# Reading the first octet of K and V in pieces of 32 KB, in a linear ReLU attention kernel

## Chip, cores and metric

The kernel runs on one core of one Trainium2 chip. The metric is the device time of one execution in microseconds; the median of 3 runs is 126.92 us (126.89 to 127.21).

## What is computed

The inputs Q, K and V are fp32 arrays of 8 batches x 12 heads x 512 rows x 64 columns, and so is the output: 96 heads, 12.58 MB for each array.

```python
Q_feat = np.maximum(0, Q)
K_feat = np.maximum(0, K)
KV = np.einsum('bhkd,bhkv->bhdv', K_feat, V)
K_sum = np.sum(K_feat, axis=2)
numerator = np.einsum('bhqd,bhdv->bhqv', Q_feat, KV)
denominator = np.einsum('bhqd,bhd->bhq', Q_feat, K_sum)
return (numerator / (denominator[:, :, :, None] + 1e-10)).astype(np.float32)
```

## The kernel before

The 96 heads are cut into 12 octets of eight heads. One octet of one input is 1 MB of fp32 that lies in one run of DRAM; seen as 128 partitions, each partition holds 32 rows of 64 values, 8 KB. For each octet the kernel forms KV and the column sums on TensorE (`mm_kv`, L185 to L190, or `mm_kv8`, L160 to L168, for the first octet), transposes and clips Q (`transp`, `relu_q`), multiplies (`out_t`, `denom`), transposes back (`back`), divides (`norm`, L271) and stores (`store`, L277 to L287).

The loads come in two kinds.

- Q of every octet, and K and V of octets 1 to 11, are loaded by GpSimd (L97 to L105), with the cast from fp32 to bf16 made on the way. K and V come in two halves per octet, called groups, so an octet takes five such DMAs: Q 512 KB and four of 256 KB, as written. All of them are issued in one list at the start of GpSimd's program (L113 to L118): Q of octet 0 first, then K, V, K, V, Q of octet 1, and so on. GpSimd gets through the list as earlier transfers land and buffers come free.
- K and V of octet 0 (tiles `k8` and `v8`, named k_first and v_first in the profile) come as fp32 without a cast, 1 MB each. K is issued by SyncE (L111) and V by ScalarE (L112), as the first DMA of each engine.

From `k8` VectorE makes the clipped and masked bf16 operands (L152), from `v8` ScalarE (L156) and VectorE (L157) make the others; this is `prep8` (L148 to L158). TensorE's list begins with the transposes of Q of octet 0 (L208), and the 32 matmuls of `mm_kv8` (L163) come after them. Then the loop over the octets runs as written out by hand from L322 on.

SyncE's queue holds, after K of the first octet, the stores in order. Each of the first seven stores stands behind a tiny DMA (L280) that reads some rows of a K group five octets further on, so that SyncE issues the store only once that group has landed; the first store is issued at 44.02 us of the span. The last octet is stored in two halves (L285).

Of the kernel before, what the change touches and what calls it, by code (L numbers as in the profile page):

```python
# [10 lines left out]
def kernel(  # L11
# [7 lines left out]
    nc = tc.nc  # L19
    B, H, S, D = Q.shape  # L20
    assert D == 64
    P = 128
# [5 lines left out]
    RQ = S * 8 // P  # L28
# [29 lines left out]
    def view(X, f):  # L58
        return X.rearrange("b h s d -> (b h s d)").rearrange("(n p f) -> n p f", p=P, f=f)
# [43 lines left out]
    def load_q(o):  # L103
        q_sb[o] = qin.tile([P, U, 2 * D], bf16, name="q_sb")
        nc.gpsimd.dma_start(out=q_sb[o].rearrange("p u f -> p (u f)"), in_=Qr[o], single_packet=True)  # L105


    K8, V8 = view(K, RQ * D), view(V, RQ * D)
    k8 = outp.tile([P, RQ, D], fp32, name="k_first", tag="o_sb")
    v8 = outp.tile([P, RQ, D], fp32, name="v_first", tag="o_sb")  # L110
    nc.sync.dma_start(out=k8.rearrange("p r d -> p (r d)"), in_=K8[0])  # L111
    nc.scalar.dma_start(out=v8.rearrange("p r d -> p (r d)"), in_=V8[0])  # L112
    load_q(0)  # L113
    make_identity(nc, ident)
    for o in range(1, NO):
# [277 lines left out]
```

## Time and profile before

The profiled execution has a span of 125.2 us from its first to its last instruction; the median of the timed runs is 1.7 us above that span.

| what | value |
|---|---|
| median of 3 runs | 126.92 us |
| span of the profiled execution | 125.2 us |
| busy: TensorE / VectorE / ScalarE | 84.8 / 83.4 / 80.8 us (68% / 67% / 65%) |
| VectorE starts on K of the first octet (L152) | 9.55 us |
| ScalarE begins its part on V of the first octet (L156) | 9.77 us |
| TensorE starts on Q of the first octet (L208) | 10.75 us |
| GpSimd issues its ninth load (L99) | 10.99 us |
| SyncE issues the first store | 44.02 us |
| last multiplication of VectorE ends (L271) | about 120.4 us |

Times of instructions count from the start of the span. In the profile's section on queues, q0 is GpSimd's queue, q1 SyncE's and q10 ScalarE's; q8 and q14 fetch instructions. A queue's share is the time that its packets took, added up, over 16 DMA engines times the length shown. The trace also keeps queue, start, size and time taken of every single DMA packet; it does not name the DMA engine of a packet. Where one packet ends and another starts at the same moment, they are taken to be of one engine.

### The profile page before, as it was taken

Reading aid. Unit: us, or ns where it says so; the run is one execution under the profiler, and the core shown is the slowest. Engines: PE = TensorE matmul, PEld = TensorE weight load, DVE = VectorE, ACT = ScalarE, POOL = GpSimd, SP = SyncE. Lnnn points to the kernel's source line nnn. Section 1 sums busy time; section 2 is a strip of 40 time slices with the busy share of each in tenths; the row PEclk is TensorE's granted clock in tenths of the full one; section 3 lists DMA queues with packets and bytes.
Section 4 is the critical chain, followed back from the end, with each engine's and each line's share of the span. In section 5 each row is a group of like instructions: output and inputs, shape, how many; then the busy total and the mean of one; then the engine's idle time right before and its main releaser. Section 6 shows DMA issues by size and latency. Waiting matters only on the chain.

```text
span 125.2 us, 2668 instructions
## 1 busy us (share of the span) xinstructions
PE 84.8 (68%) x1067; PEld 76.4 (61%) x1067; DVE 83.4 (67%) x192; ACT 80.8 (65%) x112; POOL 32.4 (26%) x62
## 2 busy tenths in 40 slices
PE   0005768497989898893598596199867767797800
PEld 0005548487978787791597494199766566696600
DVE  2719727979797998789148759433946936988440
ACT  0008989789898989988348688164929828637300
POOL 6903624415344241232133124034022000000000
PEclk9999999999999999999959999657999999999997
DMA  3999999999999999999999999999999999999993
GB/s 84 387 321 209 210 210 210 216 206 220 204 215 208 208 220 316 261 214 286 297 214 274 310 213 253 332 209 218 347 234 215 326 256 215 324 416 432 419 393 141
DMA packets 10348, 32.68 MB, mean 261 GB/s; under 512 B 1248, under 2 KB 1248, under 8 KB 8672
## 3 DMA queue, kind: packets, MB, share of 16 engines
q0 software_dynamic: 8064, 17.83, 74.4%
q1 hardware_dynamic: 2128, 13.64, 27.0%
q10 hardware_dynamic: 144, 1.05, 2.1%
q8 instruction: 8, 0.13, 0.4%
q14 instruction: 4, 0.03, 0.1%
HBM read 37.75 MB, written 12.58 MB: 402 GB/s over the span
## 4 chain that ended last, share of the span: by engine, by line
DMA 56%; PE 17%; DVE 15%; POOL 3%; issue 2%; ACT 1%; DVEq 1%; POOLq 0%
DMA q_sb<-in_Q_dram 25%; DMA v_sb<-in_V_dram 19%; DMA k_sb<-in_K_dram 12%; PE ps_kv L187 9%; DVE o_sb L271 8%; PE ps_bk L265 4%; PE ps_qt L208 4%; DVE kf L173 2%; DVE vo_all L175 1%; DVE vo_all L182 1%; DVEq L388 1%; POOL q_sb L105 1%; POOL v_sb L101 1%; POOL k_sb L99 1%; ACT ot_sb L240 1%
## 5 line engine op out<-in xcount | busy, mean ns | idle before, releaser
L271 DVE TENSOR_TENSOR o_sb<-ps_bk,rec 128x1024 f32<-128x1024 f32 x24 | 28.3, 1218 | 14.5 <-PE ps_bk L265 14.5
L187 PE MATMUL ps_kv<-vo_all,kf 128*128 128x132 bf16 x352 | 26.6, 237 | 6.3 <-DVE vo_all L182 5.8
L187 PEld LDWEIGHTS <-kf 128*128 128x128 bf16 x352 | 24.3, 105 | 7.5 <-issue 3.9
L208 PE MATMUL ps_qt<-ident,q_sb 128*128 128x128 bf16 x192 | 14.4, 235 | 18.6 <-DMA q_sb<-in_Q_dram 18.6
L216 ACT ACTIVATE qt<-ps_qt 128x1024 bf16<-128x1024 bf16 x23 | 22.4, 1023 | 7.0 <-PE ps_qt L208 6.8
L197 ACT CAST kvd<-ps_kv 64x260 bf16<-64x260 f32 (+1 forms) x46 | 16.6, 360 | 15.2 <-PE ps_kv L187 14.1
L240 ACT COPY ot_sb<-ps_ot 128x1024 f32<-128x1024 f32 x24 | 24.0, 1013 | 3.2 <-PE ps_ot L238 2.3
L208 PEld LDWEIGHTS <-q_sb 128*128 128x128 bf16 x192 | 12.7, 106 | 19.8 <-DMA q_sb<-in_Q_dram 19.7
L173 DVE TENSOR_SCALAR kf<-k_sb,mask 128x1024 bf16<-128x1024 bf16 x44 | 18.4, 459 | 9.1 <-DMA k_sb<-in_K_dram 9.1
L265 PE MATMUL ps_bk<-ident,ot_sb 128*128 128x128 f32 x192 | 23.4, 276 | 0.4 <-ACT ot_sb L240 0.4
L99 POOL DMA_DIRECT2D k_sb<-in_K_dram x22 | 12.6, 573 | 36.2 <-DMA q_sb<-in_Q_dram 26.7
L265 PEld LDWEIGHTS ps_bk<-ident,ot_sb 128*128 128x128 f32 x192 | 21.2, 143 | 0.7 <-ACT ot_sb L240 0.7
L238 PE MATMUL ps_ot<-qt,kvd 128*128 128x256 bf16 x96 | 13.9, 271 | 5.1 <-DVE o_sb L271 4.3
L101 POOL DMA_DIRECT2D v_sb<-in_V_dram x22 | 12.2, 553 | 18.7 <-DMA k_sb<-in_K_dram 12.3
L238 PEld LDWEIGHTS <-kvd 128*128 128x128 bf16 x96 | 8.9, 97 | 7.8 <-issue 5.8
L175 DVE TENSOR_SCALAR vo_all<-v_sb,mask 128x1024 bf16<-128x1024 bf16 x22 | 10.7, 484 | 1.6 <-DMA v_sb<-in_V_dram 1.6
L180 ACT ACTIVATE vo_all<-v_sb,mask 128x1024 bf16<-128x1024 bf16 x10 | 11.5, 1153 | 0.2
L247 PEld LDWEIGHTS <-qt 128*128 128x128 bf16 x192 | 6.8, 96 | 4.8 <-ACT qt L216 2.0
L247 PE MATMUL ps_den<-kvd,qt 128*128 128x16 bf16 x192 | 7.3, 179 | 3.0 <-ACT kvd L167 1.7
L105 POOL DMA_DIRECT2D q_sb<-in_Q_dram x12 | 7.1, 595 | 7.9 <-DMA v_sb<-in_V_dram 4.1
L156 ACT ACT_TABLE_LOAD x1 | 1.3, 1283 | 9.8 <-DMA v_first<-in_V_dram 9.8
L182 DVE TENSOR_SCALAR vo_all<-v_sb,mask 128x1024 bf16<-128x1024 bf16 x12 | 5.7, 478 | 0.0
(32 smaller groups left out, 42.9 us busy)
## 6 DMA issues: line engine op xcount, KB each, us to landing
out_dram<-o_sb SPq DMA_DIRECT2D x11, 1024.0 KB, 8.6
q_sb<-in_Q_dram POOLq DMA_DIRECT2D x12, 512.0 KB, 14.7
k_sb<-in_K_dram POOLq DMA_DIRECT2D x22, 256.0 KB, 14.2
v_sb<-in_V_dram POOLq DMA_DIRECT2D x22, 256.0 KB, 13.3
v_first<-in_V_dram ACTq DMA_DIRECT2D x1, 1024.0 KB, 9.0
k_first<-in_K_dram SPq DMA_DIRECT2D x1, 1024.0 KB
out_dram<-o_sb SPq DMA_DIRECT2D x2, 512.0 KB, 3.7
scratch<-k_sb SPq DMA_DIRECT2D x1, 1.0 KB
```

Source lines behind the costliest of these rows:

```text
L99: nc.gpsimd.dma_start(out=k_sb[g].rearrange("p r d -> p (r d)"), in_=Kr[g], single_packet=True)
L101: nc.gpsimd.dma_start(out=v_sb[g].rearrange("p r d -> p (r d)"), in_=Vr[g], single_packet=True)
L173: nc.vector.tensor_scalar(kf[g][:, :, s, :], k_sb[g], scalar1=0.0, scalar2=mask[:, 0, s:s + 1], op0=Alu.max, op1=Alu.mult)
L187: nc.tensor.matmul(ps_kv[:, g % 2, 0:2 * (D + 2)].rearrange("p (t d) -> p t d", t=2), kf[g][:, r, :, :].rearrange("p s d -> p (s d)"), vo[ ...
L197: copy(kvd[o % NK][64 * c:64 * c + 64, 4 * gs.start + s:4 * gs.stop:2, c * D1:c * D1 + D1].rearrange("p (g t) d -> p g t d", t=2), ps_kv[6 ...
L208: nc.tensor.transpose(ps[:, u, :], q_sb[o][:, i * (U // 2) + u, :], ident)
L216: nc.scalar.activation(to, ps, Act.Relu)
L238: nc.tensor.matmul(ps[:, i], kvd[o % NK][:, h, 1:2 * D + 1], q[:, :, h, :], start=True, stop=True, skip_group_check=True)
L240: nc.scalar.copy(ot[o][:, :, 4 * j:4 * j + 4], ps.rearrange("p h u c -> p u h c"))
L247: nc.tensor.matmul(ps[:, u], qt_sb[o % NZ][:, u, :], kvd[o % NK][:, :, 0:2 * D1:2 * D1 - 1], start=True, stop=True, skip_group_check=True)
L265: nc.tensor.transpose(ps[:, 2 * v:2 * v + 2].rearrange("p c d -> p (c d)"), ot[o][:, 8 * j + v].rearrange("p h c -> p (h c)"), ident32)
L271: nc.vector.tensor_tensor(o_sb[:, rs], ps, rec[o][:, rs].unsqueeze(2).to_broadcast([P, 16, D]), op=Alu.mult)
```

## The change

Only the two DMAs of the first octet's K and V change. Before, each was described as 128 rows of 8 KB on both sides. Now the DRAM side is described as 32 rows of 32 KB, each of which holds what goes to four partitions in turn, and the SBUF side stays 128 rows of 8 KB. To have two sides of different shape in one DMA, a small helper builds the DMA instruction by hand; engines, queues and places in the program are the same. No other instruction is added, removed or moved on any engine; the lines below move down by eight.

```diff
-    nc.sync.dma_start(out=k8.rearrange("p r d -> p (r d)"), in_=K8[0])
-    nc.scalar.dma_start(out=v8.rearrange("p r d -> p (r d)"), in_=V8[0])
+    def load_wide(engine, queue, to, of):
+        side = mybir.BassSymbolicTensorAccessPattern.from_ap
+        engine.add_instruction(mybir.InstDMACopy(
+            mode="Copy", name=nc.get_next_instruction_name(), engine=engine.engine,
+            ins=[side(of, opt=False)], outs=[side(to, opt=False)], queue=queue))
+
+    WIDE = 4
+    octet = [X.rearrange("b h s d -> (b h s d)")[0:P * RQ * D].rearrange("(p f) -> p f", p=P // WIDE) for X in (K, V)]
+    load_wide(nc.sync, "qSPDynamicHW", k8.rearrange("p r d -> p (r d)"), octet[0])
+    load_wide(nc.scalar, "qActDynamicHW", v8.rearrange("p r d -> p (r d)"), octet[1])
     load_q(0)
```

## The prediction

> **What bounds the kernel now.** I read the share of the DMA engines first. In the 40 slices it is 9 or more tenths in all but the first and the last, while no compute engine is above 68% of the span. In the queue rows, the share of q0 is GpSimd's casting loads, q1 is the first K and all stores, q10 is the first V alone.
>
> ```profile
> DMA  3999999999999999999999999999999999999993
> ...
> q0 software_dynamic: 8064, 17.83, 74.4%
> q1 hardware_dynamic: 2128, 13.64, 27.0%
> q10 hardware_dynamic: 144, 1.05, 2.1%
> q8 instruction: 8, 0.13, 0.4%
> ```
>
> These rows add up to 103.9% of 16 engines' span (records overlap a little). The chain of waits agrees: DMA holds 56% of it, in one stretch from 5.05 us to the landing of an octet's Q at 80.79 us; from there compute and the last stores follow back to back. Whatever moves the landings moves the end by about as much.
>
> ```profile
> DMA 56%; PE 17%; DVE 15%; POOL 3%; issue 2%; ACT 1%; DVEq 1%; POOLq 0%
> ```
>
> Then the stage that the change touches, with the same columns (packets, MB, share) over the first 10 us of the span alone, and the engines and DMA by stretch of time (the last two columns are DMA share and GB/s):
>
> ```profile
> q1 hardware_dynamic: 144, 1.05, 29.5%
> q10 hardware_dynamic: 144, 1.05, 26.8%
> q0 software_dynamic: 125, 0.51, 25.0%
> ```
>
> ```profile
> 1.70:2.40 0.70, 0.00 (x0) 0.00 (x0) 0.22 (x4) 0.00 (x0) 0.62 (x3) 1.00 0.76 94
> 2.40:3.20 0.80, 0.00 (x0) 0.00 (x0) 0.30 (x4) 0.00 (x0) 0.80 (x3) 1.00 0.85 256
> 3.20:3.70 0.50, 0.00 (x0) 0.00 (x0) 0.16 (x3) 0.00 (x0) 0.50 (x2) 1.00 1.04 442
> 3.70:5.60 1.90, 0.00 (x0) 0.00 (x0) 1.62 (x8) 0.00 (x0) 1.90 (x5) 1.00 0.99 414
> 5.60:8.70 3.10, 0.00 (x0) 0.00 (x0) 0.88 (x13) 0.00 (x0) 0.56 (x2) 1.00 1.03 344
> ```
>
> The reader is to see that transfers run at full rate (414 to 442 GB/s) from 3.2 us on, and at 94 and 256 before. Only those 1.5 us have slack for this change to take. (From 5.6 us on GB/s falls because q0 is counted by the 4 KB that it writes for 8 KB read.)
>
> Last, who waits:
>
> ```profile
> POOL k_sb L99 <- DMA q_sb<-in_Q_dram: 26.7, 9, 4.8
> ...
> PE ps_qt L208 <- DMA q_sb<-in_Q_dram: 18.6, 5, 10.8
> ...
> ACT L156 <- DMA v_first<-in_V_dram: 9.8, 1, 9.8
> ...
> DVE kf L152 <- DMA k_first<-in_K_dram: 2.7, 1, 2.7
> ```
>
> TensorE waits for Q five times, 18.6 us in all; 10.8 of it is the start, so 7.8 us of waiting for later Q remain. A head start of compute is lost in those waits.
>
> **The change part by part.**
>
> *What is removed.* Per DMA engine, each load had 128/16 = 8 reads of 8 KB and will have 32/16 = 2 of 32 KB. Writes stay 8 of 8 KB, bytes are equal, no instruction moves on any engine. In the packet records the steady packets of both queues took 0.309 us and follow each other, queue by queue in turn, every 0.309 us. GpSimd's packets, for as many bytes read, follow every 0.3045 us; if that is what a read without its break costs, 16 packets per engine save at most 16 x 0.0045 = 0.07 us. Lower bound 0, taken 0.02.
>
> The Trainium skill ("DMA: Bandwidth & Descriptors", section "Why small descriptors are slow") counts some 3 cycles of fixed overhead for each packet. My estimate from it, with the 850 MHz of that page's section on where its peak rate comes from: 12 fewer reads x 3.5 ns = 0.04 us, and the sum would be 0.04 instead of 0.02 in this term. No row separates the two.
>
> *What the start costs now.* By the 10 us view q1's 128 packets took 29.5% x 160 = 47.2 us, at 0.309 they would take 39.6: 7.6 too many, 0.48 per engine. q10: 26.8% x 160 = 42.9, so 3.3 too many, 0.21 per engine. The packet records say where: the first K packets of eight engines start at 1.76 to 1.85 and take 0.69 to 1.25; those of the other eight start at 2.49 to 2.64 and take 0.31 to 0.44. V's first packets that start between 2.45 and 2.90 take 0.42 to 0.78, those from 2.949 on take 0.309. So V's first read is slow where K's first 8 KB ended too soon to cover it. On four engines V's took 0.72 to 0.76 and their third packet starts at 3.54 to 3.61; on the other twelve it starts at 3.20 to 3.35.
>
> *This lag is never made up.* The end packets of q0's first load come on twelve engines within 0.14 us and on four 0.34 to 0.41 later (9.99 to 10.40); on the tenth load (22.47 to 22.88) the offsets are the same. Then two instruction fetches at 24.1 us add about 0.84 to one of the four and 0.53 to one of the twelve: 0.41 and 0.06 are gone from the offsets, 1.25 and 0.59 are new (the other pairing would charge the 8 KB fetch 0.18, less than the 0.31 it took). The fetch at 35.6 us hits another laggard: 0.38 gone, a second 1.25. A load lands with its last engine, so later loads wait for these laggards.
>
> *What the change does to it.* V's first read is queued behind 32 KB of K, some 1.24 us instead of 0.31, so it is asked for long before its turn on every engine. The four laggards lose 0.76 - 0.31 = 0.45 of waiting at the most. The last engine moves from 3.61 to the 3.35 of the twelve: 0.26. After the fetches, which hit laggards, it moves by up to 0.41. I take 0.32, between the two, for the landings and so for the end. What is late next is the first K packet's own 0.69 to 1.25, which I leave at its cost. It can lose at most 0.48 (the average above) if fewer reads also mean earlier writes, and at worst gain what a bigger first piece costs (rivals); taken 0.
>
> The Trainium skill ("DMA: Bandwidth & Descriptors", section "Queues, rings and completion order") says that a DMA engine serves its queues in turn and drains a whole packet before it switches. The alternation of q1, q10 and q0 by 8 KB agrees. By it the cover for V is 1.24 us and the 0.32 holds; if an engine could switch inside a piece, V's wait would stay bare and the term would be 0.
>
> *What is moved.* With turns of 32 KB, K has landed after three turns and V after four, with one or two q0 packets between instead of four: K's data some 2 us earlier (last packets from 7.83 to 8.15 now), V's some 0.9. L152 then starts near 7.5 us, L156 near 8.9. The gain is 0: TensorE's list has Q first, which lands when all three loads' bytes are through, as now (10.75), and the later waits for Q swallow the rest. q0's wait of a microsecond is covered by the seven loads queued behind it, four of 256 KB and more before the ninth is issued at 10.99. Without that cover it would cost up to 1.2 us.
>
> *Sum.* 0.32 + 0.02 = 0.34 us off a span of 125.2, that is 124.9; with the 1.7 us between span and median, 126.92 - 0.34 = 126.58, rounded to **126.6**. About 0.3% (0.38 us) is what a measurement of this kernel can tell from no change, and this forecast stands just inside it.
>
> **The rivals.**
>
> *Both first waits go* (A+). Fewer reads per engine are written sooner, so the second eight engines start before 2.49 and K's first packets end before 3.0. For it: the two batches of eight starts, 0.7 us apart, look like a generator at work on 128 + 128 rows, now 32 + 128. Against: the number of write rows stays. Gain 0.41 to 0.41 + 0.48 = 0.89: 126.5 down to 126.0, typically 126.2.
>
> *Hidden anyway* (zero). The lag comes from something else, or a lag of the same size arises at another turn; or the pieces are cut to 8 KB again and nothing changes: 126.9, give or take 0.1.
>
> *Wide pieces stream slower* (slower). The only packets above 8 KB here are the instruction fetches of 16 KB: 0.4% x 16 x 125.2 / 8 = 1.00 us each, against 0.62 for two steady packets. At that rate a 32 KB piece takes 2.00 instead of 1.24, and four of them per engine cost 3.0 us more, all on the DMA bound start: 126.6 + 3.0 = 129.6. If each 1.00 holds one q0 packet of 0.305 in between, 0.70 remains, 1.40 per piece, 0.64 more: 127.2. It decides from 0.34/4 = 0.085 us per piece on, that is above 1.32. Against it: two 16 KB fetches delay their engine by about 0.85, an 8 KB fetch by 0.53, so the second 8 KB cost about its steady time.
>
> **How the numbers follow.** Forecast 0.32 (126.4 to 126.8; a quarter of it beyond 0.38 us), A+ 0.28, zero 0.15, slower 0.25. Faster by over 0.3%: 0.28 + 0.08 = 0.36. Within: 0.24 + 0.15 = 0.39. Slower: 0.25. The range goes from 126.0, the end of A+ (0.06 left out below), to 127.6, past the near price of the slower rival (0.12 left out above). The forecast's own range is 126.4 to 126.8.
>
> **What would show it.** In the first 10 us: q10 with 32 or 128 data packets, and its share near 16 x 8 x 0.309 = 39.6 us, 25%; more than 30% means wide pieces are slow. V's first record with no extra over its length; end packets of q0's first load within 0.15 us instead of 0.41; L152 starting near 7.5 us; the ninth load's issue from 10.99 to about 10.7, and the last L271 earlier by the same. If Q's landings do not move though the spread is gone, the step from lag to landing is wrong; if L152 comes no earlier, the turns are not of 32 KB; a new straggler among the sixteen would turn the sign.

## The result, and the profile after

The changed kernel takes 127.17 us (median of 18 runs) against 126.97 us for the kernel before beside it: ratio 1.0014, 95% interval 1.0008 to 1.0021, so 0.18 us slower (the two medians differ by 0.20). The forecast was 0.34 us faster. Both are within the 0.3% that the forecast called no change, but the sign is wrong. The experiments show a cost that the forecast has no term for, and beside it a gain of about the forecast's size that does not come from the wide pieces.

The page of the changed kernel (span 125.5 us), with the lines that answer to those of the prediction:

```profile
DMA  4799999999999999999999999999999999999983
...
q0 software_dynamic: 8064, 17.83, 74.3%
q1 hardware_dynamic: 2032, 13.64, 26.6%
q10 hardware_dynamic: 48, 1.05, 2.2%
q8 instruction: 8, 0.13, 0.4%
...
DMA 34%; DVE 30%; PE 26%; issue 4%; ACT 2%; DVEq 1%; POOLq 0%; ACTq 0%
```

q10 has 48 packets, 32 of data and 16 of end: the pieces really are 32 KB. The DMA engines are as full as before. The chain of waits reads quite differently (DMA 34% instead of 56%), with hardly any change in time. In the changed kernel it runs from the landing of the first Q at about 10.8 us through compute to the issue of a V load at 47.38 us, and through DMA from there. I read this as two chains that end nearly together: the shares then say which was last and not that the bound has moved.

The first 10 us, by queue and then by stretch (the last two columns are DMA share and GB/s):

```profile
q10 hardware_dynamic: 48, 1.05, 27.9%
q0 software_dynamic: 126, 0.52, 25.6%
q1 hardware_dynamic: 48, 1.05, 24.9%
```

```profile
1.70:2.40 0.70, 0.00 (x0) 0.00 (x0) 0.22 (x4) 0.00 (x0) 0.62 (x3) 1.00 0.70 187
2.40:3.20 0.80, 0.00 (x0) 0.00 (x0) 0.29 (x4) 0.00 (x0) 0.80 (x3) 1.00 1.33 492
3.20:3.70 0.50, 0.00 (x0) 0.00 (x0) 0.17 (x3) 0.00 (x0) 0.50 (x2) 1.00 0.00 0
```

A packet is counted where it starts, so these stretches can't be read by GB/s any more: 32 packets of 32 KB start at a few moments and then none for a while. The queue rows can: q1's share is 24.9% x 160 / 32 = 1.245 us for each 32 KB piece, four steady 8 KB packets (1.24 us). Wide pieces stream at full rate. What q10 has above that is (27.9 - 24.9)% x 160 / 16 = 0.30 us per engine, its first packets: they start at 2.10 to 2.87 us, where the kernel before had its first at 1.76. The issues show the reason, the kernel before first, then the changed one (start, length, engine):

```profile
0.74 0.40 ACTq L112 DMA_DIRECT2D v_first<-in_V_dram  x1
0.74 0.38 SPq L111 DMA_DIRECT2D k_first<-in_K_dram  x1
```

```profile
0.74 0.55 ACTq L113 DMA_DIRECT2D v_first<-in_V_dram  x1
0.74 0.59 SPq L113 DMA_DIRECT2D k_first<-in_K_dram  x1
```

Both issues start at the same moment and take 0.15 and 0.21 us longer, and the first packet comes 0.34 us later. Nor do the two loads take turns any more: V's two pieces per engine run back to back (from 2.10 and from 4.02 us), K's first starts at 5.25.

```profile
POOL k_sb L99 <- DMA q_sb<-in_Q_dram: 24.1, 8, 4.9
...
PE ps_qt L216 <- DMA q_sb<-in_Q_dram: 18.0, 5, 10.8
...
ACT L164 <- DMA v_first<-in_V_dram: 7.2, 1, 7.2
```

ScalarE gets V 2.6 us earlier (9.8 before). TensorE still waits 10.8 us for the first Q, so ScalarE's head start doesn't bring TensorE's first work forward; the later waits for Q are 18.0 - 10.8 = 7.2 us, 0.6 less than before (7.8), while the kernel is slower.

### The profile page after: what moved, and what is told of

It is laid out like the page before. It is cut to its first block, busy times and chain, and to the rows that moved or that the text cites. A ratio compares the mean times of both kernels' runs of the same rounds, so it can differ in the third digit from the quotient of the medians.

```text
span 125.5 us, 2668 instructions
## 1 busy us (share of the span) xinstructions
PE 87.0 (69%) x1067; PEld 78.3 (62%) x1067; DVE 83.3 (66%) x192; ACT 80.8 (64%) x112; POOL 32.1 (26%) x62
## 4 chain that ended last, share of the span: by engine, by line
DMA 34%; DVE 30%; PE 26%; issue 4%; ACT 2%; DVEq 1%; POOLq 0%; ACTq 0%
DMA q_sb<-in_Q_dram 20%; DMA v_sb<-in_V_dram 14%; DVE o_sb L279 13%; PE ps_kv L195 10%; PE ps_bk L273 7%; DVE kf L181 5%; PE ps_qt L216 4%; PE ps_kv L171 4%; DVE vo_all L183 3%; DVE vo_all L190 2%; DVE den L263 2%; DVE rec L267 2%; DVE own L258 2%; DVEq L396 1%; ACT ot_sb L248 1%
## 5 line engine op out<-in xcount | busy, mean ns | idle before, releaser
L195 PE MATMUL ps_kv<-vo_all,kf 128*128 128x132 bf16 x352 | 27.1, 239 | 6.2 <-DVE vo_all L190 5.8
L195 PEld LDWEIGHTS <-kf 128*128 128x128 bf16 x352 | 24.8, 107 | 7.4 <-issue 3.8
L216 PE MATMUL ps_qt<-ident,q_sb 128*128 128x128 bf16 x192 | 15.2, 243 | 18.0 <-DMA q_sb<-in_Q_dram 18.0
L216 PEld LDWEIGHTS <-q_sb 128*128 128x128 bf16 x192 | 13.4, 110 | 19.2 <-DMA q_sb<-in_Q_dram 19.1
```

Of the source, the lines that this page charges most:

```text
L195: nc.tensor.matmul(ps_kv[:, g % 2, 0:2 * (D + 2)].rearrange("p (t d) -> p t d", t=2), kf[g][:, r, :, :].rearrange("p s d -> p (s d)"), vo[ ...
L216: nc.tensor.transpose(ps[:, u, :], q_sb[o][:, i * (U // 2) + u, :], ident)
```

## The experiments

Three theories stood first. A: the hand-built DMA is prepared more slowly, so the load starts late; the pieces themselves cost nothing. B: the 32 KB pieces cost by their length. C: the start does not matter at all. Later theory A became D, below. Ratios are against the kernel before on the same chip, with 95% intervals; the runs were spread over several chips. A ratio isn't that of the two medians, which can differ from it by up to 0.1% (e7: 126.78 / 127.01 = 0.9982; e9: 127.23 / 127.13 = 1.0008). So differences between two ratios are good to about 0.15%, 0.2 us. Packet times, in us, are from the packet records of each trace, one execution each.

| kernel | first packets | second load's first | end packets of first Q load | ratio |
|---|---|---|---|---|
| before | K 1.76 | V 2.45 | 9.99 to 10.40 | 1 |
| changed | V 2.10 | K 5.25 | 10.16 to 10.44 | 1.0014 (1.0008 to 1.0021) |
| e3 both by hand, 128 rows | V 2.07 | K 5.03 | 10.31 to 10.59 | 1.0006 (0.9995 to 1.0018) |
| e4 both by hand, 64 rows | V 2.10 | K 5.27 | 10.19 to 10.46 | 1.0010 (0.9996 to 1.0023) |
| e1 V by hand, 32 rows | K 1.77 | V 4.99 | 9.90 to 10.25 | 0.9981 (0.9968 to 0.9994) |
| e2 K by hand, 32 rows | V 1.77 | K 4.92 | 9.82 to 10.24 | 0.9977 (0.9964 to 0.9989) |
| e5 V by hand, 128 rows | K 1.75 | V 4.88 | 9.86 to 10.16 | 0.9980 (0.9972 to 0.9989) |
| e6 K by hand, 128 rows | V 1.75 | K 4.89 | 9.88 to 10.20 | 0.9981 (0.9972 to 0.9991) |
| e7 no DMA by hand, V behind K on SyncE | K 1.75 | behind K | 9.91 to 10.19 | 0.9974 (0.9965 to 0.9983) |
| e8 changed, engines exchanged | K 2.08 | V 5.09 | 10.01 to 10.65 | 1.0007 (0.9998 to 1.0015) |
| e9 e7 with a small DMA ahead | K 2.25 | behind K | 10.09 to 10.81 | 1.0017 (1.0003 to 1.0030) |
| e10 both by hand, 32 rows, on SyncE | K 2.13 | V 5.64 | 10.15 to 10.48 | 0.9990 (0.9981 to 0.9998) |

**e1 and e2: one load wide, the other as before.** e1:

```diff
-    load_wide(nc.sync, "qSPDynamicHW", k8.rearrange("p r d -> p (r d)"), octet[0])
+    nc.sync.dma_start(out=k8.rearrange("p r d -> p (r d)"), in_=K8[0])
```

> K as in the kernel before (128 rows of 8 KB on both sides), V in 32 pieces of 32 KB. Theory A (the two-shaped DMA is prepared more slowly: its issuing instruction takes 0.55 to 0.59 us instead of 0.38 to 0.40, and its first packets start 0.34 us later; the pieces themselves stream at full rate): K's issue is 0.38 us again and its first packets start at 1.76 us again; V comes late but behind K, which keeps the engines busy, so V's first wait is covered. No engine lags: the last end packet of the first Q load comes near 10.15 us instead of 10.40 (before) or 10.44 (changed), and the time is about 0.2 us below before, 126.75. Theory B (the 32 KB pieces cost by their length, in turns with the other queues): half of the change's cost, 127.07. Theory C (the start does not matter, the difference comes from TensorE's clock in the last octets): no relation to the start, 126.9 to 127.2 with Q landings that do not follow the first packets.

e2 puts the library's call back for V instead:

```diff
-    load_wide(nc.scalar, "qActDynamicHW", v8.rearrange("p r d -> p (r d)"), octet[1])
+    nc.scalar.dma_start(out=v8.rearrange("p r d -> p (r d)"), in_=V8[0])
```

> V as in the kernel before, K in 32 pieces of 32 KB. Theory A: K's issue takes 0.59 us, and K's packets start at 2.1 us or later; V's 8 KB packets now come first and find nothing to cover their start, so the engines fill as late as in the changed kernel: 127.1 to 127.2. Theory B: half of the change's cost, 127.07. Theory C: no relation to the start.

e1 came as theory A had it in time (126.80 us) and in its first packets; its last end packet came at 10.25 us, expected near 10.15. e2 did not: it is as fast as e1, where 127.1 to 127.2 us were expected (measured 126.67). Its issues:

```profile
0.74 0.38 ACTq L120 DMA_DIRECT2D v_first<-in_V_dram  x1
0.74 0.59 SPq L113 DMA_DIRECT2D k_first<-in_K_dram  x1
```

Only the hand-built DMA is slow to issue, and the other goes first at 1.77 us, whichever engine it is on. It then runs its eight packets per engine without a break (1.77 to 5.33 us), since the hand-built one has no packet before 4.92. So a late DMA shows no cost in second place, and the one-sided kernels beat both the kernel before and the changed one; theory B, which has both at half the change's cost, falls.

**e3 and e4: the hand-built DMA with narrower pieces.**

```diff
-    WIDE = 4
+    WIDE = 1
```

> The hand-built DMA with 128 rows of 8 KB on both sides, all else as in the changed kernel. Theory A: same shapes, so the issue takes 0.38 to 0.40 us, K's first packets start at 1.76 us, 144 packets on each queue, V's first wait bare on some engines, time as before, 126.97 within 0.1. If the helper itself (and not the shape) made the issue slow: issue near 0.57 us and about 127.15.

e4 sets `WIDE = 2`.

> Both loads in 64 pieces of 16 KB. Theory A: the sides differ in shape again, so the issue takes 0.55 us or more and the first packets start at about 2.1 us: 127.1 to 127.2 as in the changed kernel. Theory B: the cost goes with the length of a piece, so half of it: 127.07, with first packets still late. If the issue's length follows the number of rows on both sides (64 + 128 against 32 + 128), it is about 0.1 us longer than in the changed kernel and the time 127.2 to 127.3.

```profile
0.74 0.55 ACTq L113 DMA_DIRECT2D v_first<-in_V_dram  x1
0.75 0.59 SPq L113 DMA_DIRECT2D k_first<-in_K_dram  x1
```

These are the issues of e3, with 128 rows of 8 KB on both sides as in the kernel before. They are as long as in the changed kernel, and V's first packet is at 2.07. So theory A was wrong on the reason: it is not the two shapes. (e3's time, 1.0006, can be told neither from the kernel before nor from the changed one.) As built, e3's instruction and that of the kernel before are alike in every field but one, which the library's call sets and the helper leaves out:

```
before: "queue": "qSPDynamicHW", "mode": "Copy", ..., "single_packet": false, "ant_dge_precooked": true
e3:     "queue": "qSPDynamicHW", "mode": "Copy", ..., "single_packet": false
```

e3's 8 KB packets can be set against the kernel before in the same stretches (94, 256 and 442 GB/s there):

```profile
1.70:2.40 0.70, 0.00 (x0) 0.00 (x0) 0.21 (x4) 0.00 (x0) 0.62 (x3) 1.00 0.40 47
2.40:3.20 0.80, 0.00 (x0) 0.00 (x0) 0.29 (x4) 0.00 (x0) 0.80 (x3) 1.00 0.54 174
3.20:3.70 0.50, 0.00 (x0) 0.00 (x0) 0.17 (x3) 0.00 (x0) 0.50 (x2) 1.00 1.04 442
```

By 3.7 us that is 33 + 139 + 221 = 393 KB started, against 66 + 205 + 221 = 492: 99 KB behind, 0.23 us at 430 GB/s (the rate of the kernel before from 3.6 to 5.6 us). e4's issues take 0.56 and 0.58 us, so the issue's length doesn't follow the number of rows either, and its pieces of 16 KB make no difference to 8 or 32 KB that its interval could show.

**e5 and e6: the flag alone, on one load.** Theory D: what acts is the missing flag. In first place it delays the start; in second place its packets come near 5 us, and the other load is not interrupted. Theory E: the gain of e1 and e2 comes from the 32 KB pieces. e5 is e1, and e6 is e2, with `WIDE = 1`.

> K by the library's call as in the kernel before, V by the hand-built DMA but with 128 rows of 8 KB, so that only the missing flag differs from the kernel before, and only on V. Theory D (what acts is the slow preparation of a DMA without the flag, not the width: alone in second place its packets come only near 5 us, the first load's eight packets per engine run without a break, and no first wait is bare): V's issue 0.55 us, V's first packets at 4.9 to 5.3, the last end packet of the first Q load at 10.25 us as with V wide, ratio 0.998 as with V wide (0.9981). Theory E (the gain of the one-sided kernels comes from the 32 KB pieces): V's packets come early among K's again, the last end packet at 10.40 or later, ratio 1.000 or above.

> The mirror image: V by the library's call, K by the hand-built DMA with 128 rows of 8 KB. Theory D: V's first packets at 1.77, K's at 4.9 to 5.3, last end packet near 10.25, ratio 0.998 as with K wide (0.9977). Theory E: ratio 1.000 or above.

```profile
0.74 0.54 ACTq L113 DMA_DIRECT2D v_first<-in_V_dram  x1
0.74 0.38 SPq L119 DMA_DIRECT2D k_first<-in_K_dram  x1
```

```profile
1.70:2.40 0.70, 0.00 (x0) 0.00 (x0) 0.22 (x4) 0.00 (x0) 0.62 (x3) 1.00 0.43 70
2.40:3.20 0.80, 0.00 (x0) 0.00 (x0) 0.29 (x4) 0.00 (x0) 0.80 (x3) 1.00 0.96 389
3.20:3.70 0.50, 0.00 (x0) 0.00 (x0) 0.17 (x3) 0.00 (x0) 0.50 (x2) 1.00 0.88 360
```

In e5 the stretch from 2.4 to 3.2 us, slack before at 256 GB/s, runs at 389. The three stretches together are 49 + 311 + 180 = 540 KB against 492: 48 KB ahead, 0.11 us, less than half of the 0.25 us that e5 gains, so the fuller start is not shown to be the whole of the gain. Ratios 0.9980 and 0.9981 against 0.9981 and 0.9977 with wide pieces: theory D holds here, theory E falls, and the width is worth nothing that these runs can tell, about 0.15% either way. Between e3 (1.0006) and e6 (0.9981) a single flag differs, that of V, which goes first in both: 0.25%, 0.32 us, for 0.32 us of start (2.07 against 1.75). With both intervals the 0.32 us may be anything from 0.13 to 0.51.

**e7: the gain without any hand-built DMA.**

```diff
-    nc.scalar.dma_start(out=v8.rearrange("p r d -> p (r d)"), in_=V8[0])
+    nc.sync.dma_start(out=v8.rearrange("p r d -> p (r d)"), in_=V8[0])
```

> The kernel before with one edit: V's load is issued by SyncE right behind K's instead of by ScalarE; both with the library's call and 8 KB rows. V's descriptors then queue behind K's on the same queue. If what gains is that the first load runs unbroken while the second is made ready (theory D without any flag), V's packets start only after K's on each engine, none of them waits bare, the last end packet of the first Q load comes at 10.1 to 10.25 instead of 10.40, ratio 0.998. If the order on the queues is not what counts: ratio 1.000.

```profile
0.74 0.38 SPq L111 DMA_DIRECT2D k_first<-in_K_dram  x1
1.19 0.41 SPq L112 DMA_DIRECT2D v_first<-in_V_dram  x1
```

This is the kernel before with one word changed, and it has the lowest ratio of the study, 0.9974 or 0.33 us under before (0.23 us by the medians; e1, e2, e5 and e6 can't be told from it). V is issued 0.45 us later and the kernel is none the worse for it. Once an engine's first K packet is done, four in five of its next ones take 0.307 to 0.309 us each, the longest 0.41.

**e8: which engine.** The changed kernel with the engines of the two loads exchanged:

```diff
-    load_wide(nc.sync, "qSPDynamicHW", k8.rearrange("p r d -> p (r d)"), octet[0])
-    load_wide(nc.scalar, "qActDynamicHW", v8.rearrange("p r d -> p (r d)"), octet[1])
+    load_wide(nc.scalar, "qActDynamicHW", k8.rearrange("p r d -> p (r d)"), octet[0])
+    load_wide(nc.sync, "qSPDynamicHW", v8.rearrange("p r d -> p (r d)"), octet[1])
```

> The changed kernel with the two engines exchanged: wide K issued by ScalarE, wide V by SyncE. Theory D: ScalarE's queue goes first again, so now K's packets start at 2.10 us and V's at about 5.25; the start is as late as in the changed kernel and so is the time, ratio 1.001 (1.0014 there). If it mattered which tensor comes first (VectorE and TensorE need K's operands before V's): the first octet's compute starts earlier, but the landings stay and the ratio is still 1.001; a ratio under 0.999 would say that compute at the start counts.

ScalarE's load goes first here too, and which tensor it is makes no difference that the intervals can show: L160 starts at 7.37 instead of 9.01 us, and the ratio is 1.0007 (0.9998 to 1.0015; changed 1.0008 to 1.0021).

**e9: the price of a late start, measured by itself.** e7 with a small load ahead:

```diff
+    early = consts.tile([16, 16], fp32, name="early")
+    nc.sync.dma_start(out=early, in_=K8[0][0:16, 0:16])
     nc.sync.dma_start(out=k8.rearrange("p r d -> p (r d)"), in_=K8[0])
```

> The kernel of e7 (both loads by the library's call on SyncE, V behind K), with one small DMA of 16 rows of 64 bytes issued by SyncE ahead of them, so that K's issue and its first packets come later by about one issue of SyncE, 0.4 us, with all else as in e7. If a later start of the first packets costs the time one for one, as theory D needs it: first data packets of K near 2.15 us instead of 1.75, end packets of the first Q load later by 0.3 to 0.4 us (10.5 to 10.6 instead of 10.19), ratio 0.9974 + 0.003 = 1.0005. If the start has slack and something else carries the 0.3% between e5 and e3: ratio stays at 0.9975.

```profile
0.74 0.39 SPq L112 DMA_DIRECT2D early<-in_K_dram  x1
1.19 0.41 SPq L113 DMA_DIRECT2D k_first<-in_K_dram  x1
```

K's first packet comes at 2.25 instead of 1.75 us, and the ratio goes from 0.9974 to 1.0017: 0.55 us for 0.50 us (0.34 to 0.75 by the intervals, 0.33 by the medians). It is above the 1.0005 expected, which its interval just holds, and the last end packet came later than expected too, at 10.81 us. So the start has little or no slack: most of what is lost there comes back at the end, and the runs can't tell whether it is one for one. With this and with e3 against e6, theory C falls. The granted clock doesn't carry the difference: its mean over the runs is 0.946 in both e3 and e6.

**e10: both hand-built loads on one queue.**

```diff
-    load_wide(nc.scalar, "qActDynamicHW", v8.rearrange("p r d -> p (r d)"), octet[1])
+    load_wide(nc.sync, "qSPDynamicHW", v8.rearrange("p r d -> p (r d)"), octet[1])
```

> The changed kernel's two wide, hand-built DMAs, both on SyncE, K first. Theory D: K's first packets at 2.1 us as for any first DMA without the flag, V behind it without a bare wait; the load is as late as in the changed kernel, ratio 1.000 to 1.0015. If it is the second queue that makes the changed kernel slow (two queues preparing at the same time hinder each other), one queue starts at 1.8 us and the ratio falls to 0.998.

K starts at 2.13 us and the first Q load lands as in the changed kernel (10.48 against 10.44), as theory D has it. But the ratio, 0.9990, is below the 1.000 to 1.0015 expected and its interval does not touch the changed kernel's. Theory D is 0.1 to 0.25% off here. The first Q landings do not show this difference, and what makes it is open. What differs between the two kernels is the queue of the second load and which tensor comes first. One queue instead of two goes with 0.24% less time here, without the flag, and with 0.26% less where both loads have it (e7 against the kernel before). The second gain is put down to a first load that runs unbroken; but the changed kernel's first load runs unbroken as well, so a cost of the second queue that the first packets don't show is not excluded, and no run here tests it.

## Why the prediction was wrong, point by point

**The bound** was right in the main: the DMA engines are 9 tenths busy or more in all but the first and last slices, and the end moves with the start, 0.32 us for 0.32 (e3 against e6) and 0.33 to 0.55 for 0.50 (e9 against e7). It is not the whole: the chain of the kernel before isn't DMA all the way from 5.05 to 80.79 us, as the prediction reads it, since TensorE's work holds it from 60.73 to 64.96; the chain of the changed kernel goes through compute from 10.79 us to 47.38; and e10, which starts 0.37 us later than the kernel before, isn't slower than it.

**The step that failed** is a term that is missing. The prediction counted the new DMA instruction as the old one ("no instruction moves on any engine") and has no term for the time at which the first packet starts. Of the start it prices only the first K packet's own length, which it leaves "at its cost ... taken 0". Nothing moves, but the instruction is another: built by hand, without a flag that the library's call sets. In first place that makes the issue 0.15 to 0.21 us longer and the first packet 0.32 to 0.34 us later (e3 against e6, changed against before), and the kernel 0.25% slower (e3 against e6). The slower rival had its place elsewhere, in the streaming of wide pieces, and is refuted: 1.245 us per piece, where it needed more than 1.32. A+ had the second eight engines start before 2.49 us; in the changed kernel ten of sixteen get their first packet after that.

**The lag of four engines** (0.32 us). In the changed kernel the four stragglers are gone, as forecast: 15 of 16 end packets of the first Q load come within 0.14 us and the last at 0.28, where the spread was 0.41. But the group as a whole is late (first end packet 10.16 against 9.99), so the load lands at 10.44 instead of 10.40, and the ninth load is issued at 11.03 us, where the forecast had about 10.7 (before 10.99). Where the first load runs unbroken and early, the first Q lands 0.20 to 0.24 us earlier and the kernel gains 0.24 to 0.33 us (e5, e6, e7). That this is so near 0.32 is in part luck: it is won in another way than forecast, the end packets still spread over 0.28 to 0.32 us there, and in e2 over 0.42, with no less gain. That the changed kernel has this gain too, under its late start, is argued from its end packets and not measured. Behind the instruction fetches near 24 us the last end packet of GpSimd's twelfth load stands at 27.61 against 27.43 us, 0.18 later, as much as the whole kernel is slower; but in e10 it stands at 27.60, and e10 isn't slower, so this agreement proves nothing.

**What covers V** was named wrongly. Not 32 KB instead of 8 KB of K in front of it, but that the second load's packets come late enough not to break into the first: 8 KB rows do as well (e5, e6, e7). The cause of the late second load differs from kernel to kernel: in e7 it is behind K in SyncE's queue; without the flag it appears near 5 us, 4.1 to 4.5 us after its issue. On two queues its earliest packet follows at once on the end of a packet of the first load (in e5 at 4.877 us, in the changed kernel at 5.248), so the records show no idle engine there. The runs don't show what a second load without the flag waits for.

**The turns.** K's operands were forecast for 7.5 us and V's for 8.9; they came in the other order, L164 on V at 7.20 and L160 on K at 9.01, because V went first and the two did not alternate. From 5.25 us on the records show turns of whole pieces: K from 5.25, one packet of q0 at 6.48, K from 6.81, q0 again at 8.03. The Trainium skill ("DMA: Bandwidth & Descriptors", section "Queues, rings and completion order") has an engine drain a whole packet before it switches queues; here the trace agrees with pieces of 32 KB. That the turns don't bring the first Q forward was right: TensorE gets it at 10.79 us, before at 10.75.

**The width itself**, taken at 0.02 us with 0.07 at the most, can't be told from zero: the pairs that differ in it alone agree within 0.04% (e1 against e5, e2 against e6), but their intervals leave about 0.15%, 0.2 us. So the 0.02 us is neither confirmed nor refuted.

In sum: 0.32 to 0.34 us lost by a late start, if it counts one for one, and 0.24 to 0.33 won by an unbroken first load, if the changed kernel has that gain in full. The net of these terms is between -0.01 and 0.10 us, and the measured 0.18 is above it; the kernels whose first load is built by hand spread from 0.9990 to 1.0014, so 0.1 to 0.2 us of the changed kernel's loss is not settled term by term.

## What to carry to other kernels

When an edit builds an instruction by hand that the library's call built before, compare the two as built, field by field, before pricing the shape that the edit is about; and in the profile compare the lengths of the issuing instructions. In a kernel that is bound by DMA from its first packet on, time lost before that packet can come back at the end, here about as much as was lost (0.32 us for 0.32, 0.33 to 0.55 for 0.50, with e10 as the exception). Two large loads that start together can hinder each other at the first packet: issue them one behind the other on one queue and compare.

## What was not expected of the hardware

The time from the start of the issue to the first packet is 1.0 us with the flag (0.74 to 1.76) and 1.33 to 1.39 without it (0.74 to between 2.07 and 2.13). A second load without the flag has its first packet at 4.88 to 5.27 us, on either engine, beside a first load with the flag or without it, when the two issues start together on two queues. And in steady run one read of 32 KB that fills four partitions takes as long as four reads of 8 KB, 1.22 to 1.25 us. The flag together with wide pieces was not tried, so what comes of a DMA that has both is left open.
